# Thirty-two adaLN dot products of layer 0 go from VectorE to GpSimd and ScalarE, one per attention score step

## The chip, the cores and the metric

The kernel runs on one core of one Trainium2 chip. The metric is the device time of one execution in microseconds. Three runs of the kernel before took 1558.09, 1558.5 and 1559.41 us; their median is 1558.5 us.

## The reference, cut to what matters

Two layers of a diffusion backbone run over 256 latent tokens and 256 context tokens with 1024 features. Each layer has a mixing part (windowed attention A, latent attention B, gated linear attention C, merged by gates and projected) and a gated ConvFFN part. Ahead of each part the tokens are normalized, scaled and shifted, and what a part gives is scaled by a gate. Shift, scale and gate come from the conditioning vectors alone:

```python
silu_c = jax.nn.silu(c)
silu_cc = jax.nn.silu(c_ctx)
mod_l = (silu_c @ w_mod[l] + b_mod[l])[:, None, :]
mod_c = (silu_cc @ w_mod[l] + b_mod[l])[None, None, :]
sh1, sc1, g1, sh2, sc2, g2 = jnp.split(mod_l, 6, axis=-1)
```

`w_mod[l]` is 1024 x 6144, so each stream needs 48 tiles of 128 features, each feature a dot product of length 1024. Tiles 0 to 15 of layer 0 are shift and scale of the mixer (made early, in another way), tiles 16 to 23 its gate, tiles 24 to 39 shift and scale of the FFN, tiles 40 to 47 the FFN's gate. The change is about tiles 24 to 39 of layer 0, for both streams: 32 dot products per partition. They are wanted at the norm after the output projection of layer 0, not before.

## The kernel before, in words

Activations are feature-major, 128 features x 512 tokens a tile, and every product of the projections runs as three float32r products of high and low parts. `load_w` (L158) loads 512 columns of weights on the SP queue (L161), ScalarE rounds them to the high part `whi` (L164), and GpSimd or VectorE subtracts it to give the low part `wlo` (L168); `lo_on_pool` sets who does. In layer 0, from the attention to the output projection, GpSimd makes all of them. The weights pass through a ring of four places. `unit` (L176) issues the three products for each of 4 or 8 blocks (L172 to L174 within `mm3`).

The order of the work is set by a scheduler that places instructions engine by engine as their inputs and places come free; it can take an instruction far ahead of its place in the program. `tc.issue_after(ins)` holds instructions back behind `ins`, but only those on the engine of `ins`. Each engine then works through its own queue in order.

Layer 0 after the C phase: `attn_run` (L718) runs 16 steps for A (windowed attention) and 16 for B (latent attention), each step a pair of heads, a stream and a half of its queries. `scores` (L725): products into the PSUM pair `s` (L735, L739), maximum over the keys on VectorE (L741, with sinks L743 and L744 for A), two exponentials with row sums on ScalarE (L750), reciprocal and scaling of the probabilities `p` on VectorE (L754, L756). `values` (L759) of the step before: transposes into the PSUM pair `t` (L772), high part on ScalarE (L776), low part on VectorE (L777), and every second step `outputs` (L788, L791). Between them lie `fills`: gates and products of the merge of branches C and A.

The function `merge` (L693) has two steps for a tile: the gate (a `unit`, then a tanh on ScalarE, L700) and the product of the branch (a `unit` of half the size, then L704 and L706 on VectorE, gate times product and the sum over branches). Its PSUM banks are the two of tag `mm`; the next but one `unit` waits until L700 or L704 has read its bank.

The adaLN dot products of layer 0 are made in three places. Tiles 16 to 23 are made by `modhalf` (L107) in halves of 512, one VectorE instruction (L116) per score step, held behind the step's maximum by `issue_after` (L745 to L747); its loads are L113. Tiles 24 to 39 are made in the loop that merges branch B (L908), by `modcol` (L98): a load of 512 KB (L101) and two VectorE instructions of 1024 elements (L104), up to three tiles per `j`, held behind L706 of that `j`. Their buffers are places of `yb_` (`q`, `kh`, `kl`) that branch B no longer wants. Tiles 40 to 47 follow in the FFN. After the loop `modsum` and `ab` (L124, L132) add the bias and form the coefficients, `load_x` (L81) reads x back, and the output projection runs (L944, L945) with the norm at its end.

Of the kernel before, what the change touches and what calls it, by code (L numbers as in the profile page):

```python
"""Two layers of a hybrid backbone (windowed GQA, MLA, bidirectional GLA, ConvFFN), feature-major on one core."""
# [15 lines left out]
D = 1024  # L17
# [15 lines left out]
def hybrid(nc, tc, I, out, dbg=None, stop=None):  # L33
# [21 lines left out]
    def pair2(tag=None):  # L55
        """two banks at once; without a tag s and t take turns"""
        alt[0] ^= tag is None
        return ps.tile([128, 2, 512], F32, tag=tag or "ts"[alt[0]], name="ps_pair", bufs=1)
# [37 lines left out]
    wmb = [8]  # L96

    def modcol(mp, l, t, both, tags=("wm", "jk")):  # L98
        """adaLN features 128t.. of both streams: a dot product per partition"""
        wm = mp.tile([128, D], F32, tag=tags[0], name="wm", bufs={"wm": wmb[0], "q": 2}.get(tags[0], 1))  # L100
        nc.sync.dma_start(wm, I["wmod"][l, t])  # L101
        for s in range(2 if both else 1):
            jk = mp.tile([128, D], F32, tag=tags[1], name="jk", bufs=1)
            V.scalar_tensor_tensor(out=jk, in0=wm, scalar=1.0, in1=sil[:, s], op0=ALU.mult, op1=ALU.mult,  # L104
                                   accum_out=MOD[l][:, s, t:t + 1])

    def modhalf(mp, l, t):  # L107
        """the same in halves, as steps to be run one by one"""
        def step(i, s, hold):
            c = slice(512 * i, 512 * i + 512)  # L110
            if s == 0:
                hold["wm"] = mp.tile([128, 512], F32, tag="wm", name="wm", bufs=2)
                nc.sync.dma_start(hold["wm"], I["wmod"][l, t][:, c])  # L113
            wm = hold["wm"]
            jk = mp.tile([128, 512], F32, tag="jk", name="jk", bufs=1) if s == 0 else wm
            V.scalar_tensor_tensor(out=jk, in0=wm, scalar=1.0, in1=sil[:, s, c], op0=ALU.mult, op1=ALU.mult,  # L116
                                   accum_out=MODH[:, i, s, t:t + 1])
        r = []
        for i in range(2):
            hold = {}  # L120
            r += [lambda i=i, s=s, hold=hold: step(i, s, hold) for s in range(2)]
        return r

    def modsum(l, wh, n=2, halves=False):  # L124
        c = slice(8 * wh, 8 * wh + 8)
        b = P(l, O_BMOD + 8 * wh, 8).unsqueeze(1).to_broadcast([128, n, 8])
        dst = MOD[l][:, 0:n, c]
        if halves:
            V.tensor_tensor(out=dst, in0=MODH[:, 0, :, c], in1=MODH[:, 1, :, c], op=ALU.add)
        V.tensor_tensor(out=dst, in0=dst, in1=b, op=ALU.add)  # L130

    def ab(l, sub, both=True):  # L132
        """a = norm_w * (1 + scale), b = shift"""
        w = P(l, O_NMIX if sub == 0 else O_NFFN, 8)
        for s in range(2 if both else 1):
            V.scalar_tensor_tensor(out=AB[l][:, sub, s, 0], in0=MOD[l][:, s, 8 * (3 * sub + 1):8 * (3 * sub + 1) + 8],
                                   scalar=1.0, in1=w, op0=ALU.add, op1=ALU.mult)
            V.tensor_copy(AB[l][:, sub, s, 1], MOD[l][:, s, 24 * sub:24 * sub + 8])
# [8 lines left out]
    def lo_on_pool(a, b, c=0):  # L147
        """of every b low parts a are made by GpSimd from here on, the others by VectorE"""
        lo_mix[:] = [a, b, c]
# [3 lines left out]
    def open_ring(st, name, n):  # L153
        """n more places of the ring while st lasts"""
        rings.append((st.enter_context(pool(name)), n))
        st.callback(rings.pop)
# [35 lines left out]
    def rsqrt(ss, n, inv_n):  # L192
        """r, k with r * k = 1 / sqrt(ss * inv_n + EPS): a seed from the exponent's half, a Newton step and a cubic one"""
# [16 lines left out]
    def rms_bcast(tiles, w, nfeat, c0=0, scale=1.0, hook=None):  # L210
        """per-token 1/rms of feature-major tiles, over all partitions: [128, w]"""
# [31 lines left out]
    def hmod(l, sub, k, streams, rb, new=True):  # L243
        """tile k of H = rms(x) * a + b as exact pairs; rb covers the given streams"""
# [14 lines left out]
    def norm(l, sub, s):  # L259
        """the norm of a stream; what is left of it, as a list of steps"""  # L260
        rb, _ = rms_bcast(x, T, D, T * s)
        return [lambda k=k: hmod(l, sub, k, [s], rb) for k in range(KT)]
# [3 lines left out]
    def sil_load(mp, s):  # L266
        """silu(c) = 0.5 c (1 + tanh(c / 2)), on every partition"""
        cb = mp.tile([128, D], F32, name=f"cb{s}")
        nc.sync.dma_start(cb, I["cb"][:, s])
        S.activation(sil[:, s], cb, AF.Tanh, scale=0.5)  # L270
        S.activation(cb, cb, AF.Copy, scale=0.5)
        cbs.append(cb)

    def constants():
        """what is wanted after the first products only"""
# [9 lines left out]
    def layer(l):  # L285
# [10 lines left out]
        # the first products run along k, as tiles of H come  # L296
# [5 lines left out]
        with pool(f"mods{l}") as mp:  # L302
            if not last:
# [13 lines left out]
                def mods_sum(k):  # L317
                    """shift and scale of tile k as partial sums over four column groups"""
# [13 lines left out]
                def mods_turn(k):  # L332
                    """the sums' sum, a feature per partition; a = norm_w * (1 + scale), b = shift"""
# [36 lines left out]
        def slot(i, w, dt=F32, name="xs"):  # L370
            """space of x while x rests in DRAM (first layer)"""
            if last:
                return slots.tile([128, w], dt, tag=f"s{i}", name=name)
            return base.tile([128, NTOK], dt, tag=f"x{i}", name=name)
# [4 lines left out]
        # what outlives the C phase  # L379
# [20 lines left out]
        # ================= C: gated linear attention =================  # L400
        with pool(f"c{l}") as cp:
# [3 lines left out]
            # low-rank gates: [w hi; w lo; w hi] x [c hi; c hi; c lo]  # L405
# [22 lines left out]
            # log decays, then cumulative sums from both ends of each stream  # L428
# [36 lines left out]
            # the other projections of this phase run between the levels  # L465
# [41 lines left out]
            # pair products by levels: opposite halves of blocks of 2s tokens  # L507
# [5 lines left out]
            def pairs(aa, t, q, k, n, f):  # L513
                """k's rows times q's, in blocks of n tokens by column groups; f: the block of q that block of k meets"""
# [58 lines left out]
            # states at the ends of the context  # L573
# [33 lines left out]
            # outputs, token-major, and the norm of each head  # L607
# [57 lines left out]
            # scores of a head: [q hi; q lo] x [k hi; k hi], then q hi x k lo  # L665
# [15 lines left out]
        # ================= A and B: softmax attention =================  # L681
        gp = st.enter_context(pool(f"g{l}"))
        m = [gp.tile([128, W], F32, name=f"m{j}") for j in range(KT)]
        steps_m = [f for t in range(16, 24) for f in modhalf(gp, l, t)] if not last else []
        ya_ = {}
# [7 lines left out]
        def merge(br, yh, yl, j, first):  # L693
            """branch br into tile j of the merge, as two steps: gate, product"""
# [15 lines left out]
        def lead(steps, n):  # L710
            """the steps of all pairs in turn, the first of each pair n pairs ahead"""
            k = len(steps)
            return [f for i in range(-n, k) for f in ([steps[i + n][0]] if i + n < k else []) + ([steps[i][1]] if i >= 0 else [])]
# [4 lines left out]
        def attn_run(first, prep, fills, masked, sinks):  # L718
            """pairs of heads one after the other; prep(j)() -> q, k pairs of [rows, tokens] of both heads, v of
            [128 keys, block, head, part, 64], y pair of [128, tokens], called when the scores of pair j - 1 are done;  # L720
            scores run a step ahead of the transposes"""
# [3 lines left out]
            def scores(j, sidx, qt):  # L725
# [19 lines left out]
                if steps_m:  # L745
                    with tc.issue_after(ng.ins):
                        steps_m.pop(0)()  # L747
                pts = [common.tile([128, 512], F32, tag="p", name="p", bufs=(4, 6)[l])[:, :w] for _ in range(2)]
# [159 lines left out]
        for j in range(KT):  # L908
            r = [f() for f in merge(1, *yb, j, False)][1]
            if not last:  # L910
                with tc.issue_after(r):
                    for t in range(24 + 3 * j, min(27 + 3 * j, 40)):
                        modcol(yb_, 0, t, True, ("q" if t % 3 else "kh", "kl"))
# [9 lines left out]
        # output projection and residual  # L923
# [10 lines left out]
        if last:  # L934
            # the first up-projections run on x * a and b, ahead of the norm: W (x a / rms + b) = (W x a) / rms + W b
            # (b twice, x * a: the last places of tiles of H, whose first T H itself takes once they are used)
# [29 lines left out]
        # ================= ConvFFN =================  # L966
        with pool(f"f{l}") as fp, ExitStack() as rst:
# [51 lines left out]
            # adaLN vectors still to come, a few after each pair  # L1019
# [36 lines left out]
            # the down-projections of a group of inner tiles come after those up to the third number  # L1056
# [75 lines left out]
def _tiles(w, cols):  # L1132
    """columns of w [K, N] as stationary tiles: [n, 128, K / 128 * 128]"""
# [83 lines left out]
```

## Time and profile before

| what | value |
|---|---|
| median of three runs | 1558.5 us (1558.09 to 1559.41) |
| span of the profiled execution | 1558.0 us |
| mean granted clock of TensorE, share of full speed | 0.974 |
| PE, DVE, ACT, POOL busy in the span | 93%, 78%, 52%, 45% |
| attention A and B of layer 0, us from the start | about 215 to 478 |
| merge of branch B of layer 0 | about 478 to 561 |
| the 32 dot products (L104) within that merge | 55.7 us of VectorE |

The profiled execution's own time is its span; the median of the runs stands 0.5 us above it. PE is TensorE, PEld its weight loads, DVE VectorE, ACT ScalarE, POOL GpSimd, SP the queue that issues most loads. A matmul's bar is longer than the distance to the next one, as matmuls are pipelined, so whether TensorE loses time is read from the waits in brackets and from the granted clock, not from its busy share alone.

### The profile page before, as it was taken

What the parts mean: (1) busy time and instruction counts of PE and PEld (TensorE: products, weight loads), DVE (VectorE), ACT (ScalarE), POOL (GpSimd) and SP (SyncE); (2) the same over time, 40 slices, a digit from 0 to 9 for tenths busy, and PEclk for the clock granted to TensorE, in tenths of its full rate; (3) what the DMA queues carried; (4) which work ended last, traced back from release to release, by engine and by line L of the source; (5) the groups of instructions that cost most, each with busy time, mean ns of one, the idle gap of its engine ahead of it and who ended that gap; (6) DMA issues with size and microseconds to landing.
All of it is one profiled execution on the core that took longest, in us unless ns stands there. A gap on an engine that the chain in (4) does not pass through costs nothing. (4 is left out here: it accounts for less than half of the span.)

```text
span 1558.0 us, 27777 instructions
## 1 busy us (share of the span) xinstructions
PE 1454.5 (93%) x10062; PEld 1251.7 (80%) x10062; DVE 1208.7 (78%) x2138; ACT 812.6 (52%) x1698; POOL 697.2 (45%) x558
## 2 busy tenths in 40 slices
PE   6988989999999798999999999898999899999997
PEld 4766767777887597888888888876788889999997
DVE  4689486677787968688977977878687886797886
ACT  4654345566663244534244234565467776565663
POOL 0077233332334577745744555447354444523332
PEclk9989999999999999999999999999999999999998
DMA  8411122222226555444644774442122335556553
GB/s 318 139 55 57 49 63 79 75 68 73 78 90 213 193 195 162 149 154 150 214 142 137 251 270 136 130 148 96 62 88 83 102 102 183 169 163 197 177 169 96
DMA packets 107432, 213.28 MB, mean 137 GB/s; under 512 B 12000, under 2 KB 21600, under 8 KB 106272
## 3 DMA queue, kind: packets, MB, share of 16 engines
q1 hardware_dynamic: 106608, 210.86, 41.6%
q8 instruction: 79, 1.29, 0.3%
q10 hardware_dynamic: 688, 0.66, 0.1%
q14 instruction: 57, 0.47, 0.1%
HBM read 210.42 MB, written 1.05 MB: 136 GB/s over the span
## 5 line engine op out<-in xcount | busy, mean ns | idle before, releaser
L168 POOL TENSOR_TENSOR wlo<-raw,whi 128x512 fp32r<-128x512 f32 (+1 forms) x421 | 578.2, 1382 | 667.9 <-ACT whi L164 589.1
L164 ACT CAST whi<-raw 128x512 fp32r<-128x512 f32 (+1 forms) x614 | 358.6, 597 | 294.1 <-PE ps_mm L173 117.8
L172 PE MATMUL ps_mm<-hh,whi 128*128 128x512 f32 (+1 forms) x824 | 305.1, 370 | 1.2 <-ACT gt L700 1.2
L174 PE MATMUL ps_mm<-hh,wlo 128*128 128x512 f32 (+1 forms) x824 | 298.7, 363 | 0.0
L173 PE MATMUL ps_mm<-hl,whi 128*128 128x512 f32 (+1 forms) x824 | 298.3, 362 | 0.0
L104 DVE SCALAR_TENSOR_TENSOR jk<-wm,sil 128x1024 f32<-128x1024 f32 x112 | 192.4, 1718 | 2.2 <-DMA wm<-wmod 0.6
L172 PEld LDWEIGHTS ps_mm<-hh,whi 128*128 128x128 f32 x824 | 157.6, 191 | 29.7 <-issue 2.4
L174 PEld LDWEIGHTS ps_mm<-hh,wlo 128*128 128x128 f32 x824 | 157.3, 191 | 26.0 <-issue 0.9
L173 PEld LDWEIGHTS ps_mm<-hl,whi 128*128 128x128 f32 x824 | 158.0, 192 | 23.9 <-issue 0.4
L168 DVE TENSOR_TENSOR wlo<-raw,whi 128x512 fp32r<-128x512 f32 (+1 forms) x193 | 140.5, 735 | 29.7 <-ACT whi L164 27.7
L172 PE MATMUL ps_pair<-hh,whi 128*128 128x512 f32 (+1 forms) x312 | 110.9, 355 | 0.3 <-ACT whi L164 0.3
L174 PE MATMUL ps_pair<-hh,wlo 128*128 128x512 f32 (+1 forms) x312 | 109.5, 352 | 0.4 <-DVE wlo L168 0.4
L173 PE MATMUL ps_pair<-hl,whi 128*128 128x512 f32 (+1 forms) x312 | 109.7, 352 | 0.0
L777 DVE TENSOR_TENSOR ptl<-ps_pair,pth 128x512 fp32r<-128x512 f32 (+1 forms) x96 | 57.3, 597 | 16.7 <-ACT pth L776 16.1
L172 PE MATMUL ps_mm<-ach,whi 128*128 128x256 f32 (+1 forms) x200 | 64.3, 322 | 4.0 <-ACT ach L1050 3.6
L172 PEld LDWEIGHTS ps_pair<-hh,whi 128*128 128x128 f32 x312 | 59.4, 190 | 9.7 <-ACT whi L164 1.2
L174 PEld LDWEIGHTS ps_pair<-hh,wlo 128*128 128x128 f32 x312 | 59.2, 190 | 9.4 <-DVE wlo L168 0.6
L173 PEld LDWEIGHTS ps_pair<-hl,whi 128*128 128x128 f32 x312 | 59.4, 190 | 8.5
L776 ACT CAST pth<-ps_pair 128x512 fp32r<-128x512 f32 (+1 forms) x96 | 49.5, 515 | 32.0 <-PE ps_pair L772 17.0
L173 PE MATMUL ps_mm<-acl,whi 128*128 128x256 f32 (+1 forms) x200 | 63.9, 320 | 0.0
L174 PE MATMUL ps_mm<-ach,wlo 128*128 128x256 f32 (+1 forms) x200 | 63.8, 319 | 0.0
L1045 ACT ACTIVATE th<-cy 128x512 f32<-128x512 f32 (+1 forms) x44 | 23.1, 524 | 63.4 <-DVE cy L1017 63.4
(673 smaller groups left out, 3670.3 us busy)
## 6 DMA issues: line engine op xcount, KB each, us to landing
raw<-wup SPq DMA_DIRECT2D x184, 256.0 KB, 3.0
raw<-win SPq DMA_DIRECT2D x182, 256.0 KB, 2.7
wm<-wmod SPq DMA_DIRECT2D x72, 512.0 KB, 3.9
raw<-wdn SPq DMA_DIRECT2D x88, 256.0 KB, 2.9
raw<-wbr SPq DMA_DIRECT2D x48, 256.0 KB, 2.7
raw<-wout SPq DMA_DIRECT2D x48, 256.0 KB, 2.9
wm<-wm SPq DMA_DIRECT2D x8, 1024.0 KB, 7.8
x<-xT SPq DMA_DIRECT2D x16, 256.0 KB, 4.8
```

The costliest lines, as they stand in the source:

```text
L104: V.scalar_tensor_tensor(out=jk, in0=wm, scalar=1.0, in1=sil[:, s], op0=ALU.mult, op1=ALU.mult, accum_out=MOD[l][:, s, t:t + 1])
L164: S.copy(hi[:, :ncols], raw[:, :ncols])
L168: e.tensor_tensor(out=lo[:, :ncols], in0=raw[:, :ncols], in1=hi[:, :ncols].bitcast(F32), op=ALU.subtract)
L172: mm(o, ah, bh, start=start, stop=False)
L173: mm(o, ah, bl, start=False, stop=False)
L174: mm(o, al, bh, start=False, stop=stop)
L776: S.copy(dh, tv)
L777: V.tensor_tensor(out=dl, in0=tv, in1=dh.bitcast(F32), op=ALU.subtract)
L1045: S.activation(th, g, AF.Tanh, scale=0.5)
```

## The change

A new function `modpool` makes a dot product with two instructions: GpSimd multiplies the weights with the conditioning vector (1024 elements per partition), and ScalarE copies the products in place with a running sum (`accum_out`), which is the result. The list `steps_p` has the 32 dot products of tiles 24 to 39, and each of the 32 score steps takes one of them, in the same block in which it takes its `modhalf` step. The loop that merges branch B makes no dot products any more. The new buffers (two of weights, one of products, 4 KB per partition each) lie in space that was set aside for the scratch of dynamic DMAs, whose size is set to 1024 bytes. [...] The other lines of the diff, left out here, only remove comments.

```diff
+    def modpool(mp, l, t, s, hold):
+
+        if s == 0:
+            hold["wm"] = mp.tile([128, D], F32, tag="wmp", name="wmp", bufs=2)
+            nc.sync.dma_start(hold["wm"], I["wmod"][l, t])
+        wm = hold["wm"]
+        jk = mp.tile([128, D], F32, tag="jkp", name="jkp", bufs=1) if s == 0 else wm
+        G.tensor_tensor(out=jk, in0=wm, in1=sil[:, s], op=ALU.mult)
+        S.activation(jk, jk, AF.Copy, accum_out=MOD[l][:, s, t:t + 1])
...
         steps_m = [f for t in range(16, 24) for f in modhalf(gp, l, t)] if not last else []
+        steps_p = []
+        for t in range(24, 40) if not last else []:
+            hold = {}
+            steps_p += [lambda t=t, s=s, hold=hold: modpool(gp, l, t, s, hold) for s in range(2)]
...
                 if steps_m:
                     with tc.issue_after(ng.ins):
                         steps_m.pop(0)()
+                        steps_p.pop(0)()
...
         for j in range(KT):
-            r = [f() for f in merge(1, *yb, j, False)][1]
-            if not last:
-                with tc.issue_after(r):
-                    for t in range(24 + 3 * j, min(27 + 3 * j, 40)):
-                        modcol(yb_, 0, t, True, ("q" if t % 3 else "kh", "kl"))
+            for f in merge(1, *yb, j, False):
+                f()
...
-    nc = bacc.Bacc("TRN2", target_bir_lowering=False, num_devices=1)
+    nc = bacc.Bacc("TRN2", target_bir_lowering=False, num_devices=1, dynamic_dma_scratch_size=1024)
```

## Rows read from the trace of the kernel before

**Rows 1.** The page, busy time of each engine over the span.
```profile
PE 1454.5 (93%) x10062; PEld 1251.7 (80%) x10062; DVE 1208.7 (78%) x2138; ACT 812.6 (52%) x1698; POOL 697.2 (45%) x558
```
**Rows 2.** Stretches: busy us (count) of PE, PEld, DVE, ACT, POOL; granted clock, DMA share, GB/s.
```profile
215.00:355.00 140.00, 132.60 (x670) 104.98 (x668) 103.14 (x228) 78.09 (x191) 44.73 (x36) 0.99 0.24 76
355.00:478.00 123.00, 121.22 (x658) 102.00 (x657) 93.66 (x190) 77.79 (x182) 39.42 (x33) 1.00 0.29 94
478.00:561.00 83.00, 73.97 (x312) 57.93 (x311) 74.47 (x97) 23.87 (x42) 43.67 (x25) 0.96 0.53 176
```
**Rows 3.** Groups of instructions, 478 to 561 us: busy, mean ns, idle time before.
```profile
L104 DVE SCALAR_TENSOR_TENSOR jk<-wm,sil 128x1024 f32<-128x1024 f32 x32 | 55.7, 1741 | 0.5
L168 POOL TENSOR_TENSOR wlo<-raw,whi 128x512 fp32r<-128x512 f32 x25 | 44.4, 1788 | 40.2 <-ACT whi L164 39.2 <-DMA x<-xT 0.9
```
**Rows 4.** Waits, 478 to 561 us: us in total, times, longest.
```profile
PE ps_mm L172 <- DVE gt L704: 7.8, 3, 3.2
```
**Rows 5.** Timeline of PE in the same stretch: the three waits for L704.
```profile
510.57 0.77 PE L172 MATMUL ps_mm<-ybh,whi 128*128 128x512 f32 x1 [3.19 <-DVE gt L704]
...
531.96 0.50 PE L172 MATMUL ps_mm<-ybh,whi 128*128 128x512 f32 x1 [1.77 <-DVE gt L704]
...
544.03 0.50 PE L172 MATMUL ps_mm<-ybh,whi 128*128 128x512 f32 x1 [2.79 <-DVE gt L704]
```
**Rows 6.** Short stretches, undisturbed and around these waits (columns as in rows 2).
```profile
478.00:486.00 8.00, 8.00 (x36) 6.51 (x35) 2.93 (x5) 2.98 (x5) 3.46 (x3) 1.00 0.75 275
...
510.00:514.00 4.00, 3.43 (x8) 2.76 (x9) 4.00 (x8) 1.64 (x3) 0.48 (x1) 0.58 0.64 214
...
534.00:538.00 4.00, 3.62 (x16) 2.66 (x15) 3.96 (x6) 1.83 (x4) 3.09 (x2) 1.00 0.62 201
...
542.00:546.00 4.00, 1.97 (x6) 1.61 (x7) 3.97 (x9) 0.25 (x1) 0.00 (x0) 0.85 0.64 212
546.00:550.00 4.00, 4.00 (x14) 3.14 (x14) 3.96 (x6) 2.01 (x4) 2.46 (x2) 0.73 0.22 80
```
**Rows 7.** Timelines of DVE and SP: the end of a tile's use and the next load.
```profile
309.51 0.08 DVE L116 DVE_READ_ACCUMULATOR wm<-wm,sil 128x1 f32 x1
...
309.62 0.33 SPq L113 DMA_DIRECT2D wm<-wmod  x1
...
481.92 0.43 SPq L85 DMA_DIRECT2D x<-xT  x1
```
**Rows 8.** Single lines, over the span: ns min/median/max, first and last start.
```profile
L545 POOL TENSOR_TENSOR ex<-ex,qk x28: 719/1276/1685, 85.5 to 1094.0; 128x512 f32<-128x512 f32 x14, 128x256 f32<-128x256 f32 x14
...
L271 ACT ACTIVATE cb<-cb x2: 1057/1058/1058, 38.8 to 50.8; 128x1024 f32<-128x1024 f32 x2
```
**Rows 9.** Timeline of ACT in a score step: exponentials and their row sums.
```profile
304.00 0.47 ACT L750 ACTIVATE p<-ps_pair,st__3080 128x256 f32<-128x256 f32 x1
304.35 0.20 ACT L750 ACTIVATION_READ_ACCUMULATOR p<-ps_pair,st__3080 128x1 f32 x1
...
357.12 0.68 ACT L750 ACTIVATE p<-ps_pair,st__3655 128x512 f32<-128x512 f32 x1
```
**Rows 10.** Timeline of PE: the scores that come next after each.
```profile
307.22 0.28 PE L735 MATMUL ps_pair<-kh,q 128*128 128x256 f32 x1
...
357.94 0.51 PE L735 MATMUL ps_pair<-kh,q 96*128 96x512 f32 x1 [1.57 <-ACT p L750]
```
**Rows 11.** VectorE beside GpSimd: L104 (ns min/median/max), an L743; L116 and L706 (busy, mean ns).
```profile
L104 DVE SCALAR_TENSOR_TENSOR jk<-wm,sil x112: 1205/1645/2324, 486.9 to 951.5; 128x1024 f32<-128x1024 f32 x112
...
221.47 1.23 DVE L743 TENSOR_TENSOR st__2259<-st__2259,nsink 128x2 f32<-128x2 f32 x1
...
L116 DVE SCALAR_TENSOR_TENSOR wm<-wm,sil 128x512 f32<-128x512 f32 x16 | 10.9, 684 | 0.1
...
L706 DVE TENSOR_TENSOR m<-m,gt 128x512 f32<-128x512 f32 x8 | 7.5, 936 | 0.1
```
**Rows 12.** The page, loads of adaLN weights: KB each, median us from issue to landing.
```profile
wm<-wmod SPq DMA_DIRECT2D x72, 512.0 KB, 3.9
```

## The prediction

> **What bounds the kernel now.** I read the page first, for the engine that fills the span: TensorE's bars cover 93% of it [rows 1], so a gain can only come from where TensorE waits or runs at a lowered clock. Then I read busy time by stretch, over the part of layer 0 that the change touches [rows 2]. In the two attention stretches (215 to 478 us, 263 us) TensorE is covered for 253.8 us, VectorE for 196.8, ScalarE for 155.9 and GpSimd for 84.2: TensorE is the bound and the others have room. In the merge of branch B (478 to 561 us) it is the other way round: VectorE is busy 74.5 of 83 us, TensorE only 74.0, so 9.0 us of it are bare. The groups of that stretch say with what VectorE is filled: 55.7 us of the 74.5 are the 32 dot products of L104 [rows 3]. The waits say whom it holds up: TensorE waited 7.8 us in three pieces for L704 [rows 4], because L704 reads the PSUM bank that the next but one unit needs and stands in VectorE's queue behind up to six dot products. The timeline places the three at 510.57, 531.96 and 544.03 us [rows 5]. Short stretches around them show what comes after: behind the 3.19 us wait the granted clock was 0.58 over 4 us, behind the 2.79 us wait 0.85 and then 0.73, and behind the 1.77 us wait it stayed 1.00 [rows 6]; full speed is 2.4 GHz, the lower level 1.2.
>
> **What is removed.** The 32 dot products leave VectorE, which keeps 74.5 - 55.7 = 18.8 us of work in that stretch. L704 then runs when its product is done. TensorE gets back the three waits, 7.8 us, and what the clock cost: (0.42 + 0.15 + 0.27) x 4 us = 3.4 us. That is 11.2 us. The other bare time (9.0 - 7.8 = 1.2 us) is behind L700 on ScalarE and may stay or go, so the gain is 11.2 to 12.4 us; I take the middle, 11.8. GpSimd's low parts in this stretch took 1788 ns each [rows 3], and should come nearer to the 1276 ns of a 512-element product [rows 8]; they were not waited for, so this is worth nothing.
>
> **What is added, engine by engine.** *GpSimd:* no product of 1024 elements stands in the trace. L545 takes 1276 ns for 512 and 719 ns for 256 [rows 8]; going on at 557 ns per 256 gives 2.4 us, twice the 512 gives 2.55. I take 2.5 us, so 32 of them are 80 us, and GpSimd goes from 84 to 164 of 263 us. Behind a product wait the low parts of the ring. Undisturbed, TensorE does 36 matmuls in 8 us [rows 6]. A place of weights is worth 12, so three places ahead are some 8 us between a place's filling and its use, and 2.5 us are hidden; without that cover it would be up to 2.5 us for each of 32.
> *ScalarE:* a pass over 1024 elements takes 1058 ns [rows 8]; reading a sum takes 0.20 us, of which 0.1 overlaps [rows 9]: 1.15 us each, 37 us in all, 156 to 193 of 263 us.
> *SP and the loads:* sixteen loads of 512 KB move from the merge to the attention, past the ring's own on the same queue. One of them lands in 3.9 us [rows 12]. 8.4 MB over 263 us are 32 GB/s beside 76 to 94, with the DMA engines' share at 0.24 to 0.29 [rows 2]: free. A load that waits for its buffer holds the ring load behind it, for at most one product and one sum (3.7 us), which the same 8 us cover.
> *The instructions' place in TensorE's path:* a row sum in front of a step's exponentials delays the exponentials, which free the scores' only PSUM pair, for which the next scores wait. The timelines give this distance for 31 of the 32 steps. It is 304.47 to 307.22 us, 2.75 us, in one [rows 9, 10], and the narrowest is 357.80 to 357.94, where TensorE had waited already [rows 9, 10]. Seven are under 1.5 us (0.14, 0.15, 0.62, 0.63, 0.72, 1.01, 1.38: 4.65 us together), seven between 2.5 and 3.1 (20.3 together), seventeen above 3.5. A delay of d in every step costs what of d goes beyond these distances. With d = 1.15, the row sum alone, that is 3.6 us.
> *VectorE held up:* L104 takes 1205 ns at best and 2324 at worst, and L743, an instruction of two elements, once took 1.23 us, with a low part of some 1.3 us on GpSimd [rows 8, 11]. So an instruction with two SBUF inputs is held by a GpSimd one, and a product can hold it for 0 to 2.3 us. L706, which reads two SBUF tiles, averages 936 ns, and L116, of the same size and unhindered here, 684 [rows 11], so 0.25 us beside 1.3 us of GpSimd; a product is twice as long, so I take 0.5 us, nearest to that row. Then d = 1.65 and the cost is 7 x 1.65 - 4.65 = 6.9 us.
> The scheduler sees the new instructions and can move matmuls of the fills between, so the cost may be 0; the held-up time at its upper end gives 23.4 us (below). I take 5.2 us, the middle of 3.6 and 6.9.
>
> The Trainium skill, "GPSIMD Engine Reference", section Engine selection, speaks against the change: elementwise products belong on VectorE, GpSimd being about twice as slow. The page's 4497 ns for 2048 elements makes an estimate of 2.25 us for 1024. By that rule alone 32 x (2.25 - 1.74) = 16 us would be lost, L104 taking 1.74 us [rows 3], and it decides only where GpSimd ends last.
>
> **The sum.** 1558.0 - 11.8 + 5.2 = 1551.4 us for the profiled execution; the runs' median stands 0.5 us above it, so 1551.9.
>
> **The rivals.** *All of the gain, no cost:* the schedule closes over the new work. For it: attention B shows TensorE covered 121.2 of 123 us [rows 2]. Against: the seven narrow steps. 1558.5 - 11.8 = 1546.7 us.
> *Not one per step:* the block holds back only instructions on VectorE, and `modpool` has none there. A load goes out when its buffer is free: the buffer's last use ends at 309.59 and its load starts at 309.62 [rows 7]; and x is read back at 481.92, while seven of the eight merge tiles that precede it in the program are still to come [rows 7]. So the products may run ahead, two per step, and all fall into attention A, whose 16 steps hold three of the narrow distances and five of the middle ones as well as both engines' added work. With d = 2 x 1.65 = 3.3 there, these cost about 9.5 us: 1558.5 - 11.8 + 9.5 = 1556.2 us, which a measurement cannot tell from no change (0.2%, 3.1 us).
> *Slower, VectorE held for whole products:* a product starts ahead of a step's maximum or scaling, the two-input instruction that follows waits for most of 2.5 us, and exponentials and scores after it. Its place is the score step; d = 1.15 + 2.3 = 3.45 us; price (24.15 - 4.65) + (24.15 - 20.25) = 23.4 us; 1558.5 - 11.8 + 23.4 = 1570.1 us. It decides from d = 2.3 us, a hold of 1.2 us per step, where 7d - 4.65 reaches 11.8. For it: the 1.23 us of L743, nearly a whole low part. Against: maximum and L777 read PSUM and were not stretched in these steps, and L706's mean hold is a quarter.
> The Trainium skill, "SBUF — State Buffer", section Who interferes with whom, has this as a rule: the port pair that VectorE shares with GpSimd is locked for a whole instruction and the loser waits in full. L104 and L743 agree with it [rows 11]; by that rule the hold is decided by who starts first.
>
> **How the numbers follow.** Forecast 0.40, all of the gain 0.15, not one per step 0.20, slower 0.25. Faster by over 0.2% are the first two, 0.55; within it the third, 0.20; slower 0.25. The range leaves out half of the slower case and a little below the full gain: 1545 to 1567 us. Faster and slower cases both have weight; the forecast's own range is 1549 (cost 3) to 1555.
>
> **What would show it.** Right: no wait of TensorE for L704 and a granted clock near 1.00 from the start of branch B's merge to its end, and that stretch some 71 us instead of 83; VectorE's busy time there near 19 us; in the attention 80 us more on GpSimd and 37 on ScalarE, and the stretch 263 to 270 us long. Products spread over A and B, or bunched in A, decide between forecast and third case. Wrong: the merge as long as before, with another name on the waits; or new waits of TensorE for the exponentials (L750), the scaling (L756) or the low parts of p (L777) that add up to 12 us or more, or low parts of weights waited for.

## The result, and the profile after

The changed kernel took 1600.06 us (median of 4 runs, 1597.85 to 1602.93) where the kernel before, on the same chip, took 1558.95 us (1558.09 to 1560.52). The ratio is 1.0263 (95% interval 1.0245 to 1.0280): 41 us slower, where the forecast was a gain, and above its range. The profiled execution has a span of 1600.4 us and a mean granted clock of 0.964, where the kernel before had 0.974.

Line numbers have moved: the maximum is now L755, the sinks L757 and L758, the exponentials L765, the sum with the sinks L768, the scaling of `p` L771, the transposes L787, high and low part of `p` L791 and L792, the outputs L803 and L806, the merge's L704 and L706 are L718 and L720, and `modpool` is L131 (GpSimd) and L132 (ScalarE).

The page of the changed kernel, its line of busy times (its counterpart is [rows 1]) and the line of the granted clock in 40 slices of 40 us:

```profile
PE 1473.1 (92%) x10062; PEld 1266.9 (79%) x10062; DVE 1213.5 (76%) x2074; ACT 846.1 (53%) x1762; POOL 762.7 (48%) x590
...
PEclk9989998889999999999999999999999999999999
```

No engine has become a bound: over the span VectorE is busy 76% instead of 78%, and GpSimd 48% instead of 45%. The new thing is the 8s in slices 7 to 9, from 240 to 360 us (the 8 in slice 3 was there before). The stretches, cut where attention A, attention B and the merge of branch B end in this kernel (columns as in [rows 2]), show the place:

```profile
215.00:409.00 194.00, 154.17 (x691) 119.84 (x690) 157.80 (x242) 116.35 (x265) 125.54 (x68) 0.89 0.31 98
409.00:521.00 112.00, 111.81 (x599) 94.30 (x598) 87.26 (x179) 69.96 (x167) 35.49 (x30) 0.98 0.25 78
521.00:600.00 79.00, 78.47 (x362) 64.25 (x361) 29.39 (x32) 29.11 (x52) 36.27 (x29) 1.00 0.39 119
```

Attention A takes 194 us where it took 140 [rows 2]. TensorE is bare for 39.8 us of it (before: 7.4), 32.4 us more, and the clock of 0.89 instead of 0.99 costs 0.11 x 194 - 0.01 x 140 = 20 us at most, as part of the lowered clock fell in bare time. The two add up to some 52 of the 54 us, and the stretch holds 21 matmuls more than before. B and the merge are 11 and 4 us shorter, with 59 matmuls fewer in B and 50 more in the merge, so the gain lies in the merge; it has become what the forecast wanted: TensorE covered, clock 1.00, no wait for `gt` left. The first output product of layer 0 is added to `x` at 599.35 us and was at 561.15; so 38.2 of the span's 42.4 us have arisen by then, 1.4 of them ahead of attention A. The other 4 us come later, where the program is the same; what makes them was not looked into.

The group of L131, in the whole span (ns min/median/max, first and last start), tells where the products went:

```profile
L131 POOL TENSOR_TENSOR jkp<-wmp,sil x16: 2355/2396/2862, 227.1 to 348.3; 128x1024 f32<-128x1024 f32 x16
L131 POOL TENSOR_TENSOR wmp<-wmp,sil x16: 2338/2387/2804, 229.9 to 352.2; 128x1024 f32<-128x1024 f32 x16
```

All 32 lie in the first ten of the 16 steps of attention A, one to seven per step, none in B. The list of TensorE's waits from 215 to 409 us (us in total, times, longest) names who is late:

```profile
PE ps_o L803 <- ACT pth L791: 15.7, 6, 4.7
PE ps_pair L787 <- DVE ptl L792: 14.6, 4, 5.4
PE ps_pair L749 <- ACT p L765: 4.6, 3, 2.2
PE ps_o L806 <- DVE ptl L792: 3.5, 3, 2.9
```

Before, the same list over both attentions had no entry above 2.4 us. The timeline of one score step shows why (start, us, engine; idle time before in brackets):

```profile
229.95 2.72 POOL L131 TENSOR_TENSOR wmp<-wmp,sil 128x1024 f32<-128x1024 f32 x1
230.45 2.24 DVE L757 TENSOR_TENSOR st__2327<-st__2327,nsink 128x2 f32<-128x2 f32 x1
232.62 0.68 DVE L116 SCALAR_TENSOR_TENSOR wm<-wm,sil 128x512 f32<-128x512 f32 x1
232.63 2.86 POOL L131 TENSOR_TENSOR jkp<-wmp,sil 128x1024 f32<-128x1024 f32 x1
233.23 2.29 DVE L758 TENSOR_TENSOR st__2327<-st__2327,nsink 128x2 f32<-128x2 f32 x1
235.58 2.37 POOL L131 TENSOR_TENSOR wmp<-wmp,sil 128x1024 f32<-128x1024 f32 x1
236.15 2.35 DVE L662 TENSOR_TENSOR q<-araw,q 64x512 fp32r<-64x512 f32 x1
238.35 2.36 POOL L131 TENSOR_TENSOR jkp<-wmp,sil 128x1024 f32<-128x1024 f32 x1 [0.40 <-ACT jkp L132]
238.53 2.20 DVE L768 TENSOR_TENSOR st__2327<-st__2327 128x2 f32<-128x2 f32 x1
240.79 2.34 POOL L131 TENSOR_TENSOR wmp<-wmp,sil 128x1024 f32<-128x1024 f32 x1
240.96 2.84 DVE L771 TENSOR_SCALAR p<-p,st__2327 128x512 f32<-128x512 f32 x2
243.73 0.68 DVE L792 TENSOR_TENSOR ptl<-ps_pair,pth 128x512 fp32r<-128x512 f32 x1
...
244.55 1.94 PE L787 MATMUL ps_pair<-cst,p 128*128 128x128 f32 x8 [5.44 <-DVE ptl L792]
```

Read the DVE lines against the POOL lines. L757, L758 and L768 work on two elements per partition; unhindered they take 0.16 us (L757 of the next step does). Here each takes 2.2 to 2.3 us and ends within 0.1 us of the end of the product beside it. L662, two SBUF inputs of 512 elements, takes 0.69 us at other places and 2.35 us here; of the two scalings in L771 one takes 0.48 and the other 2.4. VectorE gets about one such instruction through between two products, and the next one waits for the next product. It goes the other way too: L116, which also has two SBUF inputs, starts at 232.62, just ahead of the product at 232.63, and takes its usual 0.68 us, and that product takes 2.86 us instead of some 2.4. The four held two-input instructions of this step lose 2.1 + 2.1 + 1.7 + 2.0 = 7.9 us, L771 another 2.0. L792 reads PSUM and is not stretched, but it stands behind them in VectorE's queue, and the transposes wait 5.44 us for it. Over A, the sixteen L757, L758 and L768 together took 17.2 + 11.5 + 7.2 us more than their shortest; before, the sinks took 2.5 us more than theirs.

### The profile page after: what moved, and what is told of

Same layout as the page of the kernel before. It is cut to its first block, busy times and chain, and to the rows that moved or that the text cites. A ratio compares the mean times of both kernels' runs of the same rounds, so it can differ in the third digit from the quotient of the medians.

```text
span 1600.4 us, 27802 instructions
## 1 busy us (share of the span) xinstructions
PE 1473.1 (92%) x10062; PEld 1266.9 (79%) x10062; DVE 1213.5 (76%) x2074; ACT 846.1 (53%) x1762; POOL 762.7 (48%) x590
## 5 line engine op out<-in xcount | busy, mean ns | idle before, releaser
L178 POOL TENSOR_TENSOR wlo<-raw,whi 128x512 fp32r<-128x512 f32 (+1 forms) x421 | 563.5, 1347 | 640.2 <-ACT whi L174 574.0
L104 DVE SCALAR_TENSOR_TENSOR jk<-wm,sil 128x1024 f32<-128x1024 f32 x80 | 137.8, 1723 | 2.9 <-DMA wm<-wmod 1.8
L792 DVE TENSOR_TENSOR ptl<-ps_pair,pth 128x512 fp32r<-128x512 f32 (+1 forms) x96 | 57.3, 597 | 21.7 <-ACT pth L791 21.2
L791 ACT CAST pth<-ps_pair 128x512 fp32r<-128x512 f32 (+1 forms) x96 | 49.3, 513 | 36.5 <-PE ps_pair L787 18.4
L787 PE MATMUL ps_pair<-cst,p 128*128 128x128 f32 x320 | 47.8, 293 | 17.1 <-DVE ptl L792 16.4
```

The costliest lines, as they stand in the source:

```text
L178: e.tensor_tensor(out=lo[:, :ncols], in0=raw[:, :ncols], in1=hi[:, :ncols].bitcast(F32), op=ALU.subtract)
L787: nc.tensor.transpose(tp[:, i, c], pts[i][:, c], ident)
L791: S.copy(dh, tv)
L792: V.tensor_tensor(out=dl, in0=tv, in1=dh.bitcast(F32), op=ALU.subtract)
```

## The experiments

Each time stands beside runs of the kernel before on the same chip, and "over the kernel before" is the difference to those. The first four and e6 have one run each, and runs of one kernel differ by several us (the kernel before beside e12 from 1554.15 to 1566.89, e7 from 1556.15 to 1571.21), so a few us between single runs show nothing. The last subsection compares the stretch that the change touches within the traces. Beside the first four the kernel before took 1561.46 us, beside the later ones 1561.26 us (e5 to e8), 1560.28 us (e9 to e11) and 1562.92 us (e12). A time "over e1" is the difference of two such differences.

### The change in parts: e1 to e4

e1 leaves all 32 dot products out:

```diff
-                        steps_p.pop(0)()
```

> Leaves out the 32 dot products of tiles 24 to 39 altogether (their results are set to zero at the start); nothing takes their place in the score steps. It measures the first term of the sum alone. All theories expect the same: attention of layer 0 as in the kernel before, the merge of branch B some 71 us instead of 83, and a time 11 to 13 us under the kernel before, about 1546 us. If it is within 3 us of the kernel before, the waits for L704 were not worth what was put down for them.

It took 1544.35 us, 17.1 under the kernel before. Not all of this belongs to the change. From the first score of attention A to the first output product of layer 0 that is added to `x`, the trace has 216.8 to 561.2 us before (344.4) and 215.3 to 546.0 in e1 (330.7). The gain in the stretch itself is thus 13.7 us, where the forecast had 11.8; the rest of the 17.1 us lies where the program is the same. The merge of B in e1 (columns as in [rows 2]):

```profile
478.00:546.00 68.00, 67.48 (x306) 54.98 (x305) 24.47 (x25) 23.89 (x43) 32.36 (x25) 1.00 0.33 109
```

TensorE is bare for 0.5 us instead of 9.0, and the clock of 1.00 instead of 0.96 over 83 us [rows 2] is worth 3.3 us. The two make 11.8 of the 13.7 us; the other 1.9 us were not traced.

e2 has the products and not the row sums:

```diff
-        S.activation(jk, jk, AF.Copy, accum_out=MOD[l][:, s, t:t + 1])
```

> Leaves out the row sums on ScalarE; loads and products on GpSimd stay (the results are set to zero). Theory 1 (a product on GpSimd holds VectorE's instructions with two SBUF inputs for its whole length, and products that follow one another hold one after the other): most of the loss stays, 1580 to 1600 us, and instructions of VectorE on two elements still take over 2 us in attention A. Theory 2 (row sums in ScalarE's queue wait for their products and hold the exponentials and the high parts of p): the loss is gone, 1546 to 1555 us. Half and half would be 1565 to 1580 us.

It took 1596.14 us, 51.8 over e1. So nearly all of the loss is there with no new work on ScalarE at all. TensorE's waits of e2 in attention A:

```profile
PE ps_pair L787 <- DVE ptl L792: 17.1, 2, 15.6
PE ps_o L806 <- DVE ptl L792: 15.3, 6, 5.6
PE ps_pair L787 <- DVE p L771: 8.1, 1, 8.1
PE ps_o L803 <- ACT pth L791: 4.4, 2, 3.6
```

Without the sums, VectorE is nearly the only name on them. In the changed kernel the largest entry read ScalarE's L791: L791 stands there behind row sums that wait for products, and behind L792, which frees its place. The name in a wait is the last link of the chain, not its cause.

e3 has the row sums and not the products (the sums read the loaded weights):

```diff
-        G.tensor_tensor(out=jk, in0=wm, in1=sil[:, s], op=ALU.mult)
-        S.activation(jk, jk, AF.Copy, accum_out=MOD[l][:, s, t:t + 1])
+        S.activation(jk, wm, AF.Copy, accum_out=MOD[l][:, s, t:t + 1])
```

> Leaves out the products on GpSimd; the row sums on ScalarE read the loaded weights instead, so both sums of a tile wait for its load only. Theory 1: the loss is gone, 1546 to 1556 us, and VectorE's instructions on two elements take 0.16 us again. Theory 2: only what waiting for products cost is gone, sums that stand in front of the exponentials still cost: 1555 to 1575 us.

It took 1549.52 us, 5.2 over e1, but this is not the price of the row sums. From the first score (216.5 us) to the first output product (544.5) e3 takes 328.0 us, 2.7 less than e1; the 5.2 us arise behind that, where both run the same program. Alone, the row sums and the loads cost nothing that these runs show; the forecast had 3.6 us for the sums.

e4 replaces each product by three fills that keep GpSimd for some 2.5 us and read nothing from SBUF:

```diff
-        G.tensor_tensor(out=jk, in0=wm, in1=sil[:, s], op=ALU.mult)
+        for w in (1024, 1024, 512):
+            G.memset(jk[:, :w], 0.5)
```

> In place of each product GpSimd fills the same buffer with a constant in three instructions (1024, 1024 and 512 elements, together about 2.5 us by the 0.53 us that a fill of 512 takes), so GpSimd is busy as long, reads nothing, and the row sums wait for it as for a product. Theory 1 (what GpSimd reads holds VectorE): 1550 to 1572 us, VectorE's instructions with two SBUF inputs not stretched. Theory 2, or that GpSimd's time itself is short and the low parts of the weights come late: about 1600 us as with the products.

It took 1566.06 us, 21.7 over e1 where the products cost 51.8, sums included here and not there. Single lines of e4 (ns min/median/max, start), the sum with the sinks (L769) and the scaling (L772) of two steps:

```profile
L769 DVE TENSOR_TENSOR st__2329<-st__2329 x1: 160/160/160, 229.4 to 229.4; 128x2 f32<-128x2 f32 x1
L769 DVE TENSOR_TENSOR st__2574<-st__2574 x1: 160/160/160, 254.4 to 254.4; 128x2 f32<-128x2 f32 x1
...
L772 DVE TENSOR_SCALAR p<-p,st__2329 x2: 1191/2221/3251, 230.3 to 231.4; 128x512 f32<-128x512 f32 x2
L772 DVE TENSOR_SCALAR p<-p,st__2574 x2: 1842/3691/5540, 254.8 to 256.5; 128x512 f32<-128x512 f32 x2
```

Fills leave the two-input instruction alone: 160 ns here, and over all sixteen steps of A L769 lost 0.2 us; beside products such instructions took 2.2 to 2.3 us. They do hold the scaling, which has one tile as input and takes 0.48 us unhindered: up to 5.54 us, longer than the three fills of a product together (six GpSimd instructions ran beside that one, a low part of weights of 1.46 us and five fills). So it matters whether GpSimd reads, and there are two kinds of hold. The Trainium skill, "SBUF — State Buffer", section Who interferes with whom, says that an instruction with two SBUF inputs contends with a GpSimd instruction that reads SBUF and not with one that only writes, and lists `tensor_scalar` among those whose faster modes take the shared ports; these rows agree with both.

### Shorter or spread holds: e6, e5, e9, e10, e12

e6 cuts each product into two halves, so that a hold is half as long:

```diff
-        G.tensor_tensor(out=jk, in0=wm, in1=sil[:, s], op=ALU.mult)
+        for h in (slice(0, 512), slice(512, 1024)):
+            G.tensor_tensor(out=jk[:, h], in0=wm[:, h], in1=sil[:, s, h], op=ALU.mult)
```

> Each product is made in two instructions of 512 elements, bunched as in the changed kernel; GpSimd's time is the same (2 x 1.28 us against 2.4 us). If the length of one hold is what counts, the loss falls by about half, to some 1575 to 1585 us; if GpSimd's busy time counts, whatever its pieces, it stays at 1595 to 1605 us.

It took 1598.6 us: nothing is gained. In this one run a shorter single hold does not help while GpSimd reads for about the same time in all.

e5 spreads the products: each is held on GpSimd behind the newest low part of weights (`lastg`), one per score step.

```diff
...
                     with tc.issue_after(ng.ins):
                         steps_m.pop(0)()
+                    with tc.issue_after(lastg[0].ins):
                         steps_p.pop(0)()
```

> The same products and row sums, but each product is held on GpSimd behind the last low part of weights that the program has issued when its score step comes, so that they spread over attention A and B instead of following one another in A. Theory 1a (the loss is products that follow one another: between two instructions of VectorE with two SBUF inputs stands always the next product): most of the loss goes, 1550 to 1562 us. Theory 1b (each product costs its hold wherever it stands): it stays above 1580 us.

The products now lie between 227.7 and 509.1 us, and it took 1609.34 us (ratio 1.0315, interval 1.0287 to 1.0342): slower still, by 7 us more than the changed kernel is. ScalarE's waits of e5 from 215 to 560 us show a second cost:

```profile
ACT jkp L132 <- POOL jkp L131: 31.9, 13, 4.1
ACT wmp L132 <- POOL wmp L131: 31.2, 11, 3.8
```

In the changed kernel these two came to 14.9 us. ScalarE takes its queue in order; a row sum that is placed ahead of its product's end holds up the exponentials and high parts behind it. The next two runs try to part the two costs.

e9 is e5 without the row sums:

> As the held version (e5), each product behind the newest low part on GpSimd and so spread over both attentions, but without the 32 row sums on ScalarE (shift and scale of layer 0's FFN are zero, so its output differs). Theory A, every product costs VectorE its hold wherever it stands: 1590 to 1600 us, as with the products bunched (1596). Theory B, spread out the holds cost little, and what the held version lost is ScalarE's queue, where 63 us of row sums stand waiting for their products: 1550 to 1565 us, and TensorE's waits for exponentials and high parts of p go back to those of the kernel without the dot products.

It took 1579.56 us (ratio 1.0114, interval 1.0090 to 1.0139), 19.3 over the kernel before and so 36.4 over e1. Neither theory's number: spread out, the holds cost 36 us instead of 52, which is less, and not little.

e10 is e5 with each row sum one score step later, behind that step's exponentials:

```diff
-        S.activation(jk, jk, AF.Copy, accum_out=MOD[l][:, s, t:t + 1])
+        return lambda: S.activation(jk, jk, AF.Copy, accum_out=MOD[l][:, s, t:t + 1])
...
-                    S.activation(pts[i], sp[:, i, :w], AF.Exp, bias=st_[:, 2 + i:3 + i], accum_out=st_[:, 4 + i:5 + i])
+                    ex = S.activation(pts[i], sp[:, i, :w], AF.Exp, bias=st_[:, 2 + i:3 + i], accum_out=st_[:, 4 + i:5 + i])
+                with tc.issue_after(ex.ins):
+                    while len(late) > (1 if steps_p else 0):
+                        late.pop(0)()
```

> As the held version (e5), but the row sum of a product is issued one score step later, behind that step's exponentials, so that ScalarE never waits for a product. All of the computation is done. Theory A (holds of VectorE wherever a product stands): 1595 to 1605 us. Theory B (ScalarE's queue): some 5 us over e9, 1555 to 1570 us, and the row sums' waits for GpSimd fall from 63 us to below 10.

It took 1594.11 us (ratio 1.0214, interval 1.0184 to 1.0245). The row sums no longer wait for a product anywhere in the attentions, and against e5 (48.1 over the kernel before) e10 (33.8 over) gets 14.3 us back, ScalarE's queue less what the new place of the sums costs. The rest stays, 50.9 us over e1. Single lines of its sum with the sinks (L776), four steps in succession:

```profile
L776 DVE TENSOR_TENSOR st__2762<-st__2762 x1: 160/160/160, 285.7 to 285.7; 128x2 f32<-128x2 f32 x1
L776 DVE TENSOR_TENSOR st__2838<-st__2838 x1: 2378/2378/2378, 292.9 to 292.9; 128x2 f32<-128x2 f32 x1
L776 DVE TENSOR_TENSOR st__2917<-st__2917 x1: 161/161/161, 303.4 to 303.4; 128x2 f32<-128x2 f32 x1
L776 DVE TENSOR_TENSOR st__3030<-st__3030 x1: 2371/2371/2371, 313.7 to 313.7; 128x2 f32<-128x2 f32 x1
```

In every second step a two-element instruction loses a whole product. This was the same in seven of A's sixteen steps, and these instructions stand between the exponentials and the scaling, on the way to the transposes. One reason why e10 lies 14.5 us above e9, where the sums alone cost nothing (e3), shows in what GpSimd waited for (215 to 560 us) and in the timeline of one such step:

```profile
POOL jkp L131 <- ACT jkp L132: 59.9, 14, 6.6
...
292.58 0.20 ACT L132 ACTIVATION_READ_ACCUMULATOR jkp<-jkp 128x1 f32 x1
292.85 2.41 POOL L131 TENSOR_TENSOR jkp<-wmp,sil 128x1024 f32<-128x1024 f32 x1 [3.44 <-ACT jkp L132]
292.90 2.38 DVE L776 TENSOR_TENSOR st__2838<-st__2838 128x2 f32<-128x2 f32 x1 [1.60 <-ACT st__2838 L775]
```

`jkp` has one buffer, so a product into it waits until the late sum has read the one before. It then starts as that sum ends, right behind the exponentials, just ahead of L776. L776 lost 17 us in e10 and its counterpart 2 us in e9; the scalings of A lost 26 and 8. No run tried whether a second buffer brings the difference back.

e12 is e9 with fills for products, as e4 has them:

> As the held products without row sums (e9), but each product is replaced by three fills of 1024, 1024 and 512 elements, which keep GpSimd for 2.7 us instead of 2.4 us and read no SBUF (the 32 dot products and their results are left out). If the 35 us of the held products come from GpSimd's time, low parts of weights queued behind the products, it takes as long as e9 or longer: 1578 to 1585 us. If they come from VectorE's instructions with two SBUF inputs, held while GpSimd reads, fills cost only what they hold of the scaling of p: 1548 to 1565 us (bunched, fills cost 22 us of the products' 52).

It took 1557.47 us (ratio 0.9974, interval 0.9953 to 0.9995), 5.5 under the kernel before. GpSimd is busy as long as in e9. The stretch 215 to 480 us (columns as in [rows 2]), e9 first:

```profile
215.00:480.00 265.00, 231.74 (x1155) 185.12 (x1155) 211.96 (x372) 140.28 (x336) 154.58 (x94) 0.95 0.31 101
```

and e12:

```profile
215.00:480.00 265.00, 249.41 (x1280) 202.68 (x1279) 198.99 (x411) 151.15 (x365) 157.35 (x162) 0.97 0.33 105
```

GpSimd's 155 and 157 us are nearly equal; TensorE gets 125 matmuls further in e12. So low parts of weights queued behind products are not the cost: with GpSimd as full, 11.7 of the 36.4 us over e1 remain, and 25 us vanish with the reads.

### The dot products back on VectorE: e7, e8, e11

e7 keeps the place of the change, one dot product per score step, and puts it back on VectorE as one instruction:

```diff
-        G.tensor_tensor(out=jk, in0=wm, in1=sil[:, s], op=ALU.mult)
-        S.activation(jk, jk, AF.Copy, accum_out=MOD[l][:, s, t:t + 1])
+        V.scalar_tensor_tensor(out=jk, in0=wm, scalar=1.0, in1=sil[:, s], op0=ALU.mult, op1=ALU.mult,
+                               accum_out=MOD[l][:, s, t:t + 1])
```

> The 32 dot products stay whole on VectorE (1.2 us each), one per score step, held behind the step's maximum; GpSimd and ScalarE get nothing. Theory 1: with no product on GpSimd the place alone costs little, VectorE goes to some 89% in the attention, 1548 to 1556 us. If the score steps have no room for anything on VectorE either, 1560 us or more.

It took 1564.43 us (ratio 1.0025, interval 1.0002 to 1.0048): all of e1's gain is eaten up, and 3 us more. A dot product takes 1217 ns there, against 1741 ns in the merge of the kernel before [rows 3]. But both attentions lose. In A the clock is 0.96 instead of 0.99 and 641 matmuls are done instead of 670; in B TensorE is now bare, 114.59 us covered instead of 121.22 [rows 2]:

```profile
215.00:355.00 140.00, 131.07 (x641) 103.56 (x640) 116.73 (x254) 76.03 (x185) 42.79 (x35) 0.96 0.37 110
355.00:478.00 123.00, 114.59 (x597) 93.62 (x597) 113.61 (x206) 74.26 (x173) 36.31 (x31) 0.99 0.32 97
```

e11 takes them back to the merge of B, but evenly, two tiles per pass instead of three for five passes and one in the sixth:

```diff
-                    for t in range(24 + 3 * j, min(27 + 3 * j, 40)):
+                    for t in (24 + 2 * j, 25 + 2 * j):
```

> All 32 dot products back on VectorE in the merge of branch B, as before the change, but two tiles (four dot products) per pass of the loop instead of three for the first five passes and one in the sixth. If the cost of the kernel before was the queue of six dot products in front of L704, about 1546 to 1551 us; if any dot product between the merge's VectorE steps costs, 1556 to 1560 us as before.

It took 1558.83 us (ratio 0.9993, interval 0.9975 to 1.0012), no change. Its list of waits in the merge still has the old name; four dot products in a row are too many as well:

```profile
PE ps_mm L182 <- DVE gt L718: 7.6, 4, 4.0
```

e8 takes half: a dot product in every second score step, and one tile per pass of the merge, all on VectorE (the products as in e7).

```diff
-        for t in range(24, 40) if not last else []:
+        for t in range(24, 32) if not last else []:
...
-                        steps_p.pop(0)()
+                        if qt == 1:
+                            steps_p.pop(0)()
...
-            for f in merge(1, *yb, j, False):
-                f()
+            r = [f() for f in merge(1, *yb, j, False)][1]
+            if not last:
+                with tc.issue_after(r):
+                    modcol(yb_, 0, 32 + j, True, ("q" if j % 3 else "kh", "kl"))
```

> All 32 dot products on VectorE, 16 of them one per second score step (tiles 24 to 31), 16 in the merge of branch B, one tile per merge tile (tiles 32 to 39) instead of up to three. The merge then has 18.8 + 16 x 1.7 = 46 us of VectorE in some 71 us, so the waits for L704 should be gone, and the score steps get half of what e7 gives them: 1545 to 1551 us, faster than the kernel before by 8 to 13 us. If up to two dot products in front of L704 are enough to hold TensorE, no better than 1553 us.

It took 1547.41 us (ratio 0.9911, interval 0.9879 to 0.9942): 13.9 us under the kernel before, 3 us from e1, which has no dot products at all, and faster than both kernels of this study. The three stretches of e8 (columns as in [rows 2]):

```profile
215.00:355.00 140.00, 131.70 (x677) 104.18 (x677) 110.24 (x248) 80.77 (x197) 43.85 (x36) 1.00 0.33 98
355.00:478.00 123.00, 122.06 (x650) 101.17 (x649) 107.20 (x205) 74.26 (x175) 39.70 (x33) 1.00 0.35 106
478.00:561.00 83.00, 81.33 (x408) 68.85 (x407) 58.90 (x69) 31.48 (x56) 46.14 (x34) 0.98 0.53 162
```

TensorE is covered in all three (A as much as before), with VectorE at 110 of 140, 107 of 123 and 59 of 83 us, and no wait for `gt` is left in the merge.

### The stretch that the change touches, in all runs

The last matter is how much of each time belongs to the change. In each trace, "first score" is the start of the first score product of attention A, "first output" the start of the first addition of an output product of layer 0 to `x`. Almost all in which the programs differ lies between the two.

| kernel | first score, us | first output, us | between, us | over e1, us |
|---|---|---|---|---|
| before | 216.8 | 561.2 | 344.4 | 13.7 |
| changed | 218.2 | 599.3 | 381.1 | 50.4 |
| e1, no dot products | 215.3 | 546.0 | 330.7 | 0 |
| e2, products alone | 216.9 | 597.9 | 381.0 | 50.3 |
| e3, row sums alone | 216.5 | 544.5 | 328.0 | -2.7 |
| e4, fills and sums | 215.7 | 567.4 | 351.7 | 21.0 |
| e6, halves | 215.9 | 596.1 | 380.2 | 49.5 |
| e5, held | 218.5 | 612.1 | 393.6 | 62.9 |
| e9, held, no sums | 215.2 | 579.5 | 364.3 | 33.6 |
| e10, held, late sums | 218.0 | 596.5 | 378.5 | 47.8 |
| e12, held fills | 216.5 | 558.5 | 342.0 | 11.3 |
| e7, VectorE, score steps | 216.9 | 565.2 | 348.3 | 17.6 |
| e11, VectorE, merge | 219.5 | 561.1 | 341.6 | 10.9 |
| e8, VectorE, both | 215.5 | 547.9 | 332.4 | 1.7 |

The large differences are as the times had them. But the row sums cost nothing here, alone (e3) or beside the products (0.1 us, changed kernel against e2); the 5.2 and 6.4 us by which those times differ lie elsewhere. Only e5, where the sums wait for their products, and e10, where products wait for the sums, lose by them.

## Why the prediction was wrong

**The gain was seen rightly.** The three waits for L704 and the clock behind them are gone, and the changed kernel's merge runs at 1.00. Forecast 11.8 us; e1 shows 13.7 in the stretch. Bare time and clock make 8.5 + 3.3 us of it, and 1.9 us were not in the rows.

**The prices of the single instructions held, the cost of their place did not.** A product was put at 2.5 us and took 2.39; a row sum at 1.15 us, and took 1.06 + 0.19 us of which 0.1 overlaps; GpSimd's low parts in the merge were to come near 1276 ns and took 1294. The row sums were to cost 3.6 us by their place in front of the exponentials, and the runs show nothing for them (e3, and the changed kernel against e2). No wait of TensorE for low parts of weights appeared, as the step on GpSimd said, and e12 bears it out.

**The order came out as the second rival had it.** The products were not one per step: `issue_after` did not hold them, and all 32 ran in A. But that was not what decided. Spread over both attentions (e9) the products cost 36 us instead of 52, and with the sums the spread kernels are nearly as slow (e10, 33.8 us over the kernel before) or slower (e5).

**The step that failed is "VectorE held up": "a product is twice as long, so I take 0.5 us, nearest to that row".** The measured cost of the products is 51.8 us (e2 against e1; 50.3 within the stretch), ten times the 5.2 us put for everything that is added. Three things were wrong in it.

First, the row. L706's mean excess of 0.25 us was taken as the hold beside a low part. That mean is over eight instructions (215 to 478 us), of which five met no GpSimd instruction and took 0.67 to 0.69 us; the three that met a low part took 1.21, 1.25 and 1.62. Two of the eight, with the low part beside the second, in the kernel before:

```profile
452.05 0.67 DVE L706 TENSOR_TENSOR m<-m,gt 128x512 f32<-128x512 f32 x1
...
475.83 1.29 POOL L168 TENSOR_TENSOR wlo<-raw,whi 128x512 fp32r<-128x512 f32 x1 [1.94 <-PE ps_o L788]
476.05 1.62 DVE L706 TENSOR_TENSOR m<-m,gt 128x512 f32<-128x512 f32 x1
```

So 0.25 us is the hold of a meeting, 0.5 to 0.9 us, times how often one came, and more work on GpSimd raises both. In the changed kernel the same instruction (L720) took 1563 ns beside low parts of 1294 ns, an excess of 0.88 us. L743's 1.23 us, which stood in the same group [rows 11], was the better row: it shows a two-element instruction losing nearly all of a low part.

Second, the count. The sum had one held instruction per step, and the slower rival, too, capped the hold at one product, 2.3 us. The step shown above has five held ones, 9.9 us together, because the products follow one another within 0.4 us. So the slower rival had the right mechanism and the right sign with a chance of 0.25, and its 23.4 us were still less than half of the loss. The rule of the Trainium skill that stood beside it ("SBUF — State Buffer", section Who interferes with whom), that the loser waits in full, is borne out by L757, L758 and L768 there, each of which ends with the product beside it.

Third, the clock. It stood in the gain and not in the cost. The new waits in A took the clock from 0.99 to 0.89, and up to 20 of the 54 us that A grew are that.

**The sum as measured, within the stretch:** -13.7 us (e1), +50.3 (products, e2) and +0.1 (row sums beside them) make 36.7 of the changed kernel's 41.1 us; the other 4.4 lie where the program is the same, and their cause is open. What was to show the forecast wrong has come: waits of TensorE for the low parts of `p` (L777, now L792), 14.6 us from one line. The largest entry, for the high parts (L791), was not among the names given.

## What to carry to other kernels

Before work is moved to GpSimd, count the VectorE instructions beside it that have two SBUF inputs, however small, and, where GpSimd's instructions read SBUF and follow one another, price each at up to a whole one of them; in this case neither their size nor the engine's busy share told it. Where one stretch has an engine too full, look first at how its work can be dealt out over all stretches in which that engine has room: half of the dot products at each of two places was worth 14 us, all of them at either place nothing. And a cost in new waits is to be counted with the clock that falls behind them, as a gain is.

## What was not expected of the hardware

Halving the products changed nothing (1598.6 us against 1600.06). Between two products about one held instruction of VectorE came through, so that an instruction of two elements took 2.2 to 2.4 us, some fifteen times its 0.16 us. Fills, which read no SBUF, left such instructions at 160 ns, but stretched a scaling of 512 elements with one SBUF tile as input from 0.48 to 5.54 us, over five fills and a low part, none longer than 1.46 us; bunched, the fills cost some 21 us (e4 against e1). The same dot product took 1217 ns on VectorE in the attention (e7) and 1741 to 1761 ns in the merge beside low parts of weights ([rows 3], e8).
